# Log-sum-exp on one core: 112 rows per partition plus 16 read last, a small final store, and a logarithm held behind row 118

## Chip, cores, metric

One core of one Trainium2 chip. The metric is device microseconds of one execution; medians are over the runs of one kernel on one chip. "Column" below means one row of x in each of the 128 partitions: 128 x 4 KB, 0.524 MB. There are 128 columns.

## The reference

```python
x: [32, 512, 1024] float32, standard normal
max_x = np.max(x, axis=-1, keepdims=True)
return max_x.squeeze(-1) + np.log(np.sum(np.exp(x - max_x), axis=-1))
```

67.1 MB are read and 64 KB written. The kernel skips the maximum, sums the plain exponentials, and tests with a flag whether that was safe; the slow branch behind the flag is not taken here.

## The kernel before

Columns stream through a ring of 48. ScalarE takes the exponential. Then there are three ways to sum a column: R (VectorE reduces several columns in one instruction), T (VectorE adds the two halves and accumulates), A (ScalarE accumulates while it takes the exponential). One string of the list is one load step.

```python
B = 8                                   # columns of the second layout
W = NC - B                              # 120 rows of x, contiguous, in each partition
x_rows = x_flat[0 : P * W].rearrange("(p c) d -> p c d", p=P)
x_rest = x_flat[P * W : n].rearrange("(p c) d -> p c d", p=P)
...
loads = [
    "R8 R8", "R8 R8", "R8 R8", "R7 R6 A A", "R6 R5 A A A", "R5 R4 A", "R5 R4", "R5 T3",
    "R3 A A A", "R3 A", "R2 T2", "R3", "R1 A", "T2", "T1", "A", "A",
]
REST = 7                                # step 7 reads x_rest: columns 0 to 7
...
if following == EARLY + 14:             # logarithm of 104 columns; the scheduler places it
    nc.scalar.activation(out=res[:, 0:EARLY], in_=sumexp[:, 0:EARLY], func=AF.Ln)
if following == LATE + 3:
    check(0, LATE, 0)
...
nc.scalar.activation(out=res[:, EARLY:NC], in_=sumexp[:, EARLY:NC], func=AF.Ln)
nc.sync.dma_start(out=out_rest, in_=res[:, 0:B])        # 4 KB, early
nc.sync.dma_start(out=out_rows, in_=res[:, B:NC])       # 60 KB, last
```

## Time and profile before

| | before |
|---|---|
| device time, first measurement | 163.82 us (163.78 to 163.91) |
| span in the profile | 162.0 us |
| DMA engines busy | 97.0% |
| VectorE busy, ScalarE busy | 122.4 us, 116.8 us |
| ScalarE takes up the first and the last load | 22.04 us, 158.16 us |
| final store: issue, size | 159.58 us, 60 KB |

From the first load taken up to the last one taken up are 158.16 - 22.04 = 136.12 us, and I use this difference as the pace of the stream. What comes after 158.16 is a fixed tail. The first landing, the pace and the tail make up the span. The profile's own lines are in the prediction.

### The profile page before, as it was taken

To read this page: it belongs to the slowest core of one execution; us is meant where nothing else is said; L and a number is where in the kernel's file an instruction comes from. 1 tells how busy PE (TensorE), PEld (TensorE's weight loads), DVE (VectorE), ACT (ScalarE), POOL (GpSimd) and SP (SyncE) were. 2 spreads that over 40 slices of the span, in tenths; PEclk is the share of its full clock that TensorE was granted. 3 is DMA by queue.
4 is the path that set the end of the run, shared out by engine and by line. 5 is a ranking of instruction groups with operands and counts; after the bars stand their busy time and mean duration, and the time that the engine had idled before them with its cause. 6 is when DMAs were issued, how large, how long until landed. Compare 5 with 4: busy or idle time off the path is not lost.

```text
span 162.0 us, 216 instructions
## 1 busy us (share of the span) xinstructions
PE 0.6 (0%) x8; PEld 0.3 (0%) x8; DVE 122.4 (76%) x47; ACT 116.8 (72%) x53; POOL 0.2 (0%) x4
## 2 busy tenths in 40 slices
PE   0000000000000000000000000000000000000001
PEld 0000000000000000000000000000000000000000
DVE  0000000899949999499999995999998999979993
ACT  3000059980799609994599839999969599999993
POOL 0000000000000000000000000000000000000000
DMA  8995995996996999799999899899999999999980
GB/s 275 502 518 259 518 518 259 518 518 275 502 518 291 485 502 425 303 485 485 453 453 453 382 394 425 384 453 437 437 396 469 394 455 401 425 423 417 414 350 19
DMA packets 2818, 67.19 MB, mean 415 GB/s; under 512 B 640, under 2 KB 640, under 8 KB 1024
## 3 DMA queue, kind: packets, MB, share of 16 engines
q1 hardware_dynamic: 2816, 67.18, 97.0%
q14 instruction: 2, 0.02, 0.0%
HBM read 67.11 MB, written 0.07 MB: 415 GB/s over the span
## 4 chain that ended last, share of the span: by engine, by line
DMA 63%; DVE 22%; ACT 12%; issue 0%; SPq 0%; PE 0%; DVEq 0%; ACTq 0%
DMA ring<-in_x_dram 63%; DVE sumexp L140 21%; ACT ring L133 12%; DVE ring L145 1%; SPq L90 0%; PE count L193 0%; DVE clamped L102 0%; DVE bad L190 0%; DVE bad L189 0%; DVE clamped L106 0%; DVE fine L195 0%; PE count L194 0%; DVEq L102 0%; ACTq L133 0%
## 5 line engine op out<-in xcount | busy, mean ns | idle before, releaser
L140 DVE TENSOR_REDUCE sumexp<-ring 128x8 f32<-128x8192 f32 (+7 forms) x20 | 116.2, 5854 | 36.0 <-ACT ring L133 36.0
L133 ACT ACTIVATE ring<-ring 128x8192 f32<-128x8192 f32 (+7 forms) x24 | 101.7, 4283 | 42.0 <-DMA ring<-in_x_dram 41.9
L131 ACT ACTIVATE ring<-ring 128x1024 f32<-128x1024 f32 x12 | 12.5, 1040 | 0.0
L145 DVE SCALAR_TENSOR_TENSOR ring<-ring 128x512 f32<-128x512 f32 x8 | 5.1, 683 | 0.0
L131 ACT ACTIVATION_READ_ACCUMULATOR ring<-ring 128x1 f32 x12 | 2.2, 186 | 0.0
L77 ACT ACT_TABLE_LOAD x1 | 1.3, 1283 | 0.8 <-PEq L253 0.8
L131 ACT ACTIVATE last_exp<-ring 128x1024 f32<-128x1024 f32 x1 | 1.0, 1028 | 0.0
L110 PE MATMUL count<-far,bad 128*1 128x1 f32 x4 | 0.4, 164 | 158.8 <-DVE clamped L106 158.8
L78 DVE MEMSET ones<- 128x1 f32 x1 | 0.1, 59 | 0.9 <-PEq L253 0.9
L145 DVE DVE_READ_ACCUMULATOR ring<-ring 128x1 f32 x8 | 0.6, 81 | 0.0
L102 DVE TENSOR_SCALAR clamped<-sumexp 128x118 f32<-128x118 f32 (+1 forms) x2 | 0.4, 198 | 0.1
L106 DVE SCALAR_TENSOR_TENSOR clamped<-clamped,sumexp 128x118 f32<-128x118 f32 (+1 forms) x2 | 0.4, 224 | 0.1
L110 PEld LDWEIGHTS count<-far,bad 128*1 128x1 f32 x4 | 0.2, 80 | 158.9 <-DVE clamped L106 158.9
L195 DVE TENSOR_SCALAR fine<-count 1x1 int32<-1x1 f32 x1 | 0.1, 145 | 0.3 <-PE count L194 0.3
L162 ACT ACTIVATE res<-sumexp 128x104 f32<-128x104 f32 x1 | 0.3, 272 | 0.0
L182 ACT ACTIVATE res<-sumexp 128x24 f32<-128x24 f32 x1 | 0.2, 222 | 0.0
L189 DVE TENSOR_REDUCE bad<-ring 128x1 f32<-128x64 f32 x1 | 0.2, 219 | 0.0
L193 PE MATMUL count<-far,bad 128*1 128x1 f32 x2 | 0.2, 164 | 0.2 <-DVE bad L190 0.2
L194 PE MATMUL count<-ones,sumexp 128*1 128x1 f32 x2 | 0.2, 163 | 0.0
L131 ACT ACTIVATION_READ_ACCUMULATOR last_exp<-ring 128x1 f32 x1 | 0.2, 186 | 0.0
L190 DVE TENSOR_SCALAR bad<-bad 128x1 f32<-128x1 f32 x1 | 0.2, 153 | 0.0
L106 DVE DVE_READ_ACCUMULATOR clamped<-clamped,sumexp 128x1 f32 x2 | 0.2, 82 | 0.0
(7 smaller groups left out, 0.6 us busy)
## 6 DMA issues: line engine op xcount, KB each, us to landing
ring<-in_x_dram SPq DMA_DIRECT2D x2, 3840.0 KB, 27.7
ring<-in_x_dram SPq DMA_DIRECT2D x2, 3584.0 KB, 25.6
ring<-in_x_dram SPq DMA_DIRECT2D x1, 5120.0 KB, 31.3
ring<-in_x_dram SPq DMA_DIRECT2D x1, 4608.0 KB, 33.7
ring<-in_x_dram SPq DMA_DIRECT2D x1, 4096.0 KB, 29.3
ring<-in_x_dram SPq DMA_DIRECT2D x2, 2048.0 KB, 32.7
ring<-in_x_dram SPq DMA_DIRECT2D x1, 3072.0 KB, 36.2
ring<-in_x_dram SPq DMA_DIRECT2D x2, 1024.0 KB, 38.7
```

Source lines behind the costliest of these rows:

```text
L77: nc.scalar.preload_act_table_set("natural_log_exp_and_others")
L102: nc.vector.tensor_scalar(out=clamped[:, c0:c1], in0=sumexp[:, c0:c1], scalar1=LOW, scalar2=HIGH, op0=ALU.max, op1=ALU.min,)
L106: nc.vector.scalar_tensor_tensor(out=clamped[:, c0:c1], in0=clamped[:, c0:c1], scalar=0.0, in1=sumexp[:, c0:c1], op0=ALU.bypass, op1=ALU.n ...
L110: nc.tensor.matmul(count, lhsT=bad[:, i : i + 1], rhs=far, start=i == 0, stop=False)
L131: exp = nc.scalar.activation(out=o, in_=v, func=AF.Exp, accum_out=sums)
L133: exp = nc.scalar.activation(out=v, in_=v, func=AF.Exp)
L140: added = [nc.vector.reduce_sum(out=sums, in_=v, axis=AX.X)]
L145: nc.vector.scalar_tensor_tensor(out=lo, in0=lo, scalar=1.0, in1=ring[:, p + r, H:d], op0=ALU.mult, op1=ALU.add, accum_out=sums[:, r : r + 1],
L162: nc.scalar.activation(out=res[:, 0:EARLY], in_=sumexp[:, 0:EARLY], func=AF.Ln)
L182: nc.scalar.activation(out=res[:, EARLY:NC], in_=sumexp[:, EARLY:NC], func=AF.Ln)
L189: nc.vector.reduce_max(out=bad[:, 3:4], in_=last_row[:, 0, 0 : d // 16], axis=AX.X)
L190: nc.vector.tensor_scalar(out=bad[:, 2:3], in0=bad[:, 3:4], scalar1=LOG_LOW, scalar2=None, op0=ALU.is_lt)
```

## The change

The intent: the rows that are read last become the second layout, so that 112 columns can be stored early and only 16 in the final store. The logarithm of the 112 and the check of 118 are pinned to a place in the order of their engines. The list of loads is redrawn, and there must be a border between loads at 112.

```diff
-    B = 8
+    B = 16
-        "R8 R8", "R8 R8", "R8 R8", "R7 R6 A A", "R6 R5 A A A", "R5 R4 A", "R5 R4", "R5 T3",
-        "R3 A A A", "R3 A", "R2 T2", "R3", "R1 A", "T2", "T1", "A", "A",
+        "R6 R5 R5", "R6 R5 R5", "R8 R8", "R8 R8", "R4 R4 R3 R3 A A", "R6 T3 T3", "R6 A A", "R4 T2",
+        "R3 R3", "R3", "A A A", "R2 A", "T2", "T2", "T1", "A", "A",
...
-        if following == EARLY + 14:
-            nc.scalar.activation(out=res[:, 0:EARLY], in_=sumexp[:, 0:EARLY], func=AF.Ln)
-        if following == LATE + 3:
-            check(0, LATE, 0)
+        if c == LATE:                    # 118
+            ln = nc.scalar.activation(out=res[:, 0:W], in_=sumexp[:, 0:W], func=AF.Ln)
+            in_this_order(exp, ln)       # and ln before the next exp
+            counted = check(0, LATE, 0)  # and before the next VectorE sum
...
-    nc.sync.dma_start(out=out_rest, in_=res[:, 0:B])
-    nc.sync.dma_start(out=out_rows, in_=res[:, B:NC])
+    nc.sync.dma_start(out=out_rows, in_=res[:, 0:W])
+    nc.sync.dma_start(out=out_rest, in_=res[:, W:NC])
```

(The helper that pins an order and the slow branch's adjustments are cut.)

More of the change, by code (lines that the diff above doesn't have):

```diff
@@ L56 @@
     ENGINES = [mybir.EngineType.Activation, mybir.EngineType.DVE]
-    REST = 7
-    EARLY = 104
     LATE = 118
@@ L81, in source @@
     def source(c0, size):
-        assert c0 >= B or (c0 == 0 and size == B)
-        return x_rows[:, c0 - B : c0 - B + size, :] if c0 >= B else x_rest
+        assert c0 >= W or c0 + size <= W
+        return x_rest[:, c0 - W : c0 - W + size, :] if c0 >= W else x_rows[:, c0 : c0 + size, :]
     def load(p0, c0, size, i):
@@ L98, in without_wait, with in_this_order @@
         tc.declare_no_dep(ins.ins, group=group, reason=reason)
+    def in_this_order(first, then):
+        info = mybir.DependencyInfo(mybir.DependencyClass.NoSync, mybir.DependencyReason.DATA)
+        tc.add_manual_dep(then.ins, first.ins.name, info, reason="order on one engine")
     def check(c0, c1, i):
@@ L105, in check @@
         )
-        nc.vector.scalar_tensor_tensor(
+        counted = nc.vector.scalar_tensor_tensor(
             out=clamped[:, c0:c1], in0=clamped[:, c0:c1], scalar=0.0, in1=sumexp[:, c0:c1],
@@ L110, in check @@
         nc.tensor.matmul(count, lhsT=bad[:, i : i + 1], rhs=far, start=i == 0, stop=False)
-    following = B
+        return counted
+    ln = counted = None
+    c = 0
     p = 0
@@ L117 @@
             p = 0
-        if i == REST:
-            c = 0
-        else:
-            c = following
-            following += size
         dmas = load(p, c, size, i)
@@ L137 @@
             tc.add_to_no_dep_group("exps", exp.ins)
+            if ln:
+                in_this_order(ln, exp)
+                ln = None
             added = []
@@ L155 @@
                 tc.add_to_no_dep_group("sums", add.ins)
+                if counted:
+                    in_this_order(counted, add)
+                    counted = None
             c += s
@@ L180 @@
     nc.at_finalize(start_early)
-    nc.scalar.activation(out=res[:, EARLY:NC], in_=sumexp[:, EARLY:NC], func=AF.Ln)
-    nc.sync.dma_start(out=out_rest, in_=res[:, 0:B])
-    nc.sync.dma_start(out=out_rows, in_=res[:, B:NC])
+    nc.scalar.activation(out=res[:, W:NC], in_=sumexp[:, W:NC], func=AF.Ln)
+    nc.sync.dma_start(out=out_rows, in_=res[:, 0:W])
+    nc.sync.dma_start(out=out_rest, in_=res[:, W:NC])
     check(LATE, LAST, 1)
@@ L210 @@
                         nc.scalar.wait_ge(ready, steps)
-                    for c1, s1 in ((0, B), (B, s - B)) if c0 == 0 else ((c0, s),):
+                    edge = max(c0, min(W, c0 + s))
+                    for c1, c2 in ((c0, edge), (edge, c0 + s)):
+                        if c1 == c2:
+                            continue
                         nc.scalar.dma_start(
-                            out=ring[:, c1 - c0 : c1 - c0 + s1, :], in_=source(c1, s1)
+                            out=ring[:, c1 - c0 : c2 - c0, :], in_=source(c1, c2 - c1)
                         ).then_inc(landed, 16)
@@ L235 @@
                 nc.scalar.wait_ge(ready, steps + 2)
-                nc.scalar.dma_start(out=out_rest, in_=res[:, 0:B]).then_inc(landed, 16)
-                nc.scalar.dma_start(out=out_rows, in_=res[:, B:NC]).then_inc(landed, 16)
+                nc.scalar.dma_start(out=out_rest, in_=res[:, W:NC]).then_inc(landed, 16)
+                nc.scalar.dma_start(out=out_rows, in_=res[:, 0:W]).then_inc(landed, 16)
                 nc.scalar.wait_ge(landed, rows + 32)
```

## The prediction

> **What bounds the kernel now.** I went from the page's shares to the DMA stages, then to the last ten microseconds in order of time. The page first: each engine's busy time, the load queue, and the chain that ended last.
>
> ```profile
> span 162.0 us, 216 instructions
> PE 0.6 (0%) x8; PEld 0.3 (0%) x8; DVE 122.4 (76%) x47; ACT 116.8 (72%) x53; POOL 0.2 (0%) x4
> q1 hardware_dynamic: 2816, 67.18, 97.0%
> DMA 63%; DVE 22%; ACT 12%; issue 0%; SPq 0%; PE 0%; DVEq 0%; ACTq 0%
> ```
>
> VectorE and ScalarE have about a quarter of the span free; the 16 DMA engines have 3%, or 4.9 us, and that is the start and the end. Next, the windows view, cut where ScalarE got its next load (its columns end with GB/s).
>
> ```profile
> 22.04:41.39 19.35, 0.00 (x0) 0.00 (x0) 12.29 (x2) 13.95 (x3) 0.00 (x0) 1.00 1.00 434
> 95.89:118.87 22.98, 0.00 (x0) 0.00 (x0) 20.98 (x5) 21.70 (x12) 0.00 (x0) 1.00 0.99 428
> 135.89:154.35 18.46, 0.19 (x2) 0.09 (x2) 17.25 (x18) 18.18 (x17) 0.00 (x0) 1.00 1.00 420
> 158.16:160.30 2.14, 0.43 (x6) 0.22 (x6) 1.11 (x8) 1.37 (x4) 0.00 (x0) 1.00 0.00 0
> 160.40:160.60 0.20, 0.00 (x0) 0.00 (x0) 0.00 (x0) 0.00 (x0) 0.00 (x0) 1.00 0.72 206
> 160.60:160.80 0.20, 0.00 (x0) 0.00 (x0) 0.00 (x0) 0.00 (x0) 0.00 (x0) 1.00 0.38 101
> ```
>
> The loads run at 420 to 434 GB/s without a gap until ScalarE takes up the last one at 158.16. One column (128 rows of 4 KB, 0.524 MB) costs 19.35/16 = 1.209 us in the big loads and 18.46/15 = 1.231 us in the small ones. From 160.4 to 160.8 the final store's data moves. The tail between is a strict sequence, here from the timeline:
>
> ```profile
> 154.35 2.86 ACT L133 ACTIVATE ring<-ring 128x2048 f32<-128x2048 f32 x2 [0.24 <-DMA ring<-in_x_dram]
> 157.11 1.04 ACT L131 ACTIVATE ring<-ring 128x1024 f32<-128x1024 f32 x1
> 158.16 1.03 ACT L131 ACTIVATE last_exp<-ring 128x1024 f32<-128x1024 f32 x1
> 159.12 0.19 ACT L131 ACTIVATION_READ_ACCUMULATOR last_exp<-ring 128x1 f32 x1
> 159.34 0.22 ACT L182 ACTIVATE res<-sumexp 128x24 f32<-128x24 f32 x1
> 159.58 0.34 SPq L184 DMA_DIRECT2D out_dram<-res  x1
> 159.64 0.14 DVE L195 TENSOR_SCALAR fine<-count 1x1 int32<-1x1 f32 x1 [0.33 <-PE count L194]
> ```
>
> So the end is: last load, 1.15 us to the accumulator of its exponential, 0.25 us for the logarithm, store issued at 159.58, landed 1.6 us later (DMA issues in the page: "60.0 KB, 1.6"), span over at 162.0. The chain as printed ends in the flag test at 159.78 instead of the store, because it follows instructions; the flag's load and branch come after that, and it is done only some 0.3 us before the store has landed (the trace's semaphore records: 160.87 and 161.16), so I count it as a close second.
>
> **What the Trainium skill says.** "DMA: Bandwidth & Descriptors", section "Where 436 GB/s comes from", gives 435.2 GB/s as what the ports can take; the 434 of the big loads agrees: no arrangement of loads makes them faster. Its "Latency and other measured facts" says that a tiny transfer has a floor of about 800 ns whatever its size, and its "Specifications" that transfers under 512 B a piece are below line rate. The final store agrees with the first: 1.6 us, of which only 0.35 us has data in flight. 480 B and 64 B a row are both under 512 B, so that does not tell them apart. The same section of measured facts lists slow row pitches: 512 KiB still gives 207 GB/s against 214, 2 MiB 164. The change moves the pitch between partitions from 480 KB to 448 KB, and to 64 KB for the last sixteen columns; all are no larger than the page's mild case, so I expect no loss, but no run here has shown it.
>
> **The change, part by part.**
>
> 1. Loads. Both versions move 128 columns in 17 steps, with the same split of steps 3 to 5 among transfers and the same last five sizes (2, 2, 1, 1, 1). Between the steps of the old kernel, landing time fits 1.2045 us a column plus 0.07 us a step (estimate from the ScalarE starts: 16 columns give 19.34, and 4 give 4.89). New sum after the first step: 112 x 1.2045 + 16 x 0.07 = 136.0 us, exactly as before, since columns and steps are equal. First landing 22.02, so the last is at about 158.1 in both. Gain 0.
>
> 2. Slots of the ring. A load may be issued when VectorE has freed its 48-column ring's slots. Working the new order through with the old durations (VectorE 8.60 us for eight columns, 6.47 for six, 5.39 for five, 4.33, 3.27, 2.19; 0.61 for a T column), slots come free at 44.6, 63.9, 84.9, 95.8, 104.4 us and so on, each 9 to 30 us before the queue would run dry (60.7, 80.1, 99.4, 113.9, 123.7). Smaller first pieces free slots about 2 us earlier; with a queue that never empties that earns nothing. Gain 0.
>
> 3. Engines. VectorE: R columns 107 to 105, T columns 8 to 13, so 20 reductions and 8 additions become 21 and 13. I find six instructions more (eleven records, with accumulator reads), not the seven fewer of the description; busy time goes up about 1 us: -2.0 for the reductions (forms 8.68, 7.62, 6.55, 5.48, 4.41, 3.35, 2.28, 1.21), +5 x 0.61 = +3.1. ScalarE: A columns 13 to 10, about 1.2 us less. Neither sets the end. In the last columns my walk has VectorE finish its last addition at 158.2 (158.5 before), still ahead of ScalarE's 159.31.
>
> 4. The logarithm of 112 columns after row 118, and the check pinned there. ScalarE reaches it at about 149.4; it needs VectorE's reduction up to column 112, which my walk puts at 148.5. 0.9 us to spare, so it costs its own 0.18 us of start-to-start time (old one: 141.67 to 141.85). Afterwards ScalarE takes R2, A, T2: 149.55 + 1.82 + 1.04 + 1.82 = 154.2, against the landing of the next T2 at 154.33. It is level with the loads again, by 0.1 us. From there the sequence T2, T1, A, A is the old one: the last exponential at 158.16. Gain 0.
>
> 5. The stores. The early one (now 112 x 4 B a row, 56 KB) is issued near 149.7, but waits in the queue behind loads all issued by then, as the old one did (4.0 KB, 16.3 us to landing, that is 158.3). Its data takes about as long as the old final store's, under 0.4 us, and is gone by 158.6, a microsecond before the final store. The final store shrinks from 60 KB to 8 KB. Of its 1.6 us only the data part of 0.35 us scales: 52 KB less, at 434 GB/s, is 0.12 us; at the 150 GB/s that the old store reached (60 KB in 0.4 us) it would be 0.3 us, but the eight rows that an engine has still have a cost each. I choose 0.12. The logarithm of 16 instead of 24 columns is worth under 0.01 us. Gain 0.12.
>
> Sum: 163.82 - 0.12 = 163.70 us, or -0.07%.
>
> **Rivals.**
>
> ScalarE stalls at the pinned logarithm: if VectorE runs more than 0.9 us later than in my walk, ScalarE waits, and all but 0.1 us of the wait goes straight to the end, because the old tail has no idle ScalarE after 154.35. For it: VectorE was continuously behind in this stretch. Against it: the order of work leaves only three R3 and two T before it. A 1 us stall would make 164.6.
>
> The last sixteen columns load slower because of their 64 KB pitch. For it: nothing in the old trace reads in that pitch with 4 to 12 KB pieces. Against it: the page's figures, and the old kernel's contiguous step ran at the same 1.214 us a column as its strided neighbours. 3% on sixteen columns is 0.6 us: 164.3.
>
> The flag becomes the end: with a quicker store, the flag's branch at about 160.8 is the next wait. It would cap the gain at 0.3 us: 163.5. A full gain of a smaller store plus nothing else cannot make more than that.
>
> **Range and chances.** The old runs spread over 0.13 us, and chip and build may shift 0.2. Stall and pitch are about 1 in 8 together and cost up to 1 us; the best case is 163.4. So 163.4 to 164.1. 2% is 3.3 us. Faster by that would need bytes not moved; slower would need a rate loss of the whole stream, such as a bad 448 KB pitch: 2 in 100.
>
> **What would show it.** The chain and windows: 430 GB/s stages as before and a last exponential at 158.1 to 158.2 prove parts 1 and 2. No idle ScalarE ahead of the logarithm of 112, starting near 149.4, proves part 4. The final store's line must say 8.0 KB and about 1.5 us instead of 1.6. VectorE busy near 123.4 and ScalarE near 115.6 check part 3. I am wrong if ScalarE's last start is off by over 0.3 us, or if a gap appears in the DMA rows before 157.

## The result, and the profile after

| | before | after |
|---|---|---|
| median of 6 runs | 163.83 us (163.78 to 163.91) | 163.71 us (163.64 to 163.75) |
| ratio | 1 | 0.9992, 95% interval 0.9979 to 1.0005 |

A ratio is the mean time of one kernel's runs over that of the other's in the same rounds, so it is not quite the ratio of the medians. The 0.12 us between the medians is within the interval, although the two ranges of six runs do not overlap.

The page of the changed kernel (engine shares and load queue):

```profile
span 162.0 us, 224 instructions
PE 0.6 (0%) x8; PEld 0.3 (0%) x8; DVE 123.2 (76%) x58; ACT 116.2 (72%) x50; POOL 0.2 (0%) x4
q1 hardware_dynamic: 2816, 67.18, 96.9%
```

VectorE has eleven records more, not fewer, and 0.8 us more work; the queue is as full as before. The timeline after, from the first load and in the tail:

```profile
21.81 14.04 ACT L133 ACTIVATE ring<-ring 128x6144 f32<-128x6144 f32 x3 [19.73 <-DMA ring<-in_x_dram]
...
149.06 0.19 ACT L131 ACTIVATION_READ_ACCUMULATOR ring<-ring 128x1 f32 x1
149.15 0.28 ACT L168 ACTIVATE res<-sumexp 128x112 f32<-128x112 f32 x1
149.34 1.89 ACT L133 ACTIVATE ring<-ring 128x2048 f32<-128x2048 f32 x1
...
154.29 2.86 ACT L133 ACTIVATE ring<-ring 128x2048 f32<-128x2048 f32 x2 [0.22 <-DMA ring<-in_x_dram]
...
158.13 1.03 ACT L131 ACTIVATE last_exp<-ring 128x1024 f32<-128x1024 f32 x1
...
159.07 0.22 DVE L195 TENSOR_REDUCE bad<-ring 128x1 f32<-128x64 f32 x1 [0.42 <-issue]
...
159.55 0.34 SPq L190 DMA_DIRECT2D out_dram<-res  x1
...
159.81 0.15 DVE L201 TENSOR_SCALAR fine<-count 1x1 int32<-1x1 f32 x1 [0.33 <-PE count L200]
```

The two stores in the lists of DMA issues (KB, then us from issue to landing), of the kernel before, then of the changed one:

```profile
out_dram<-res SPq DMA_DIRECT2D x1, 60.0 KB, 1.6
out_dram<-res SPq DMA_DIRECT2D x1, 4.0 KB, 16.3
```

```profile
out_dram<-res SPq DMA_DIRECT2D x1, 56.0 KB, 8.9
out_dram<-res SPq DMA_DIRECT2D x1, 8.0 KB, 1.5
```

The pinned logarithm starts at once. ScalarE is level with the loads again at 154.29, with 0.22 us to spare. The last exponential is 0.03 us earlier than before, and so is the final store's issue. One thing is new: VectorE's small reduction has 0.42 us of "issue" ahead of it, a wait for nothing that the profile shows. The flag comes out at 159.96, not earlier, as an earlier last addition would have it, but 0.17 us later. It still does not set the end: SyncE's own semaphore records in the trace have the flag at 160.8 and the store landed at 161.08 (before: 160.87 and 161.16).

From issue to landing the final store takes 1.53 us after and 1.58 before. So this one pair of profiles shows 0.05 us of gain in the store, less than predicted, and could not settle where the 0.12 came from.

### The profile page after: what moved, and what is told of

The parts are those of the page before. It is cut to its first block, busy times and chain, and to the rows that moved or that the text cites. A ratio compares the mean times of both kernels' runs of the same rounds, so it can differ in the third digit from the quotient of the medians.

```text
span 162.0 us, 224 instructions
## 1 busy us (share of the span) xinstructions
PE 0.6 (0%) x8; PEld 0.3 (0%) x8; DVE 123.2 (76%) x58; ACT 116.2 (72%) x50; POOL 0.2 (0%) x4
## 4 chain that ended last, share of the span: by engine, by line
DMA 52%; DVE 36%; ACT 9%; issue 1%; SPq 0%; PE 0%; DVEq 0%; ACTq 0%
DMA ring<-in_x_dram 52%; DVE sumexp L143 35%; ACT ring L133 9%; DVE ring L148 1%; SPq L88 0%; DVE bad L195 0%; PE count L199 0%; DVE clamped L105 0%; DVE bad L196 0%; DVE fine L201 0%; DVE clamped L109 0%; PE count L200 0%; DVEq L195 0%; DVEq L105 0%; ACTq L133 0%
## 5 line engine op out<-in xcount | busy, mean ns | idle before, releaser
L143 DVE TENSOR_REDUCE sumexp<-ring 128x3 f32<-128x3072 f32 (+5 forms) x21 | 113.9, 5479 | 34.1 <-ACT ring L133 34.0
L133 ACT ACTIVATE ring<-ring 128x3072 f32<-128x3072 f32 (+6 forms) x27 | 104.4, 3921 | 42.5 <-DMA ring<-in_x_dram 42.5
L131 ACT ACTIVATE ring<-ring 128x1024 f32<-128x1024 f32 x9 | 9.4, 1040 | 0.0
L148 DVE SCALAR_TENSOR_TENSOR ring<-ring 128x512 f32<-128x512 f32 x13 | 8.3, 687 | 0.7 <-ACT ring L133 0.7
L131 ACT ACTIVATION_READ_ACCUMULATOR ring<-ring 128x1 f32 x9 | 1.7, 186 | 0.0
L148 DVE DVE_READ_ACCUMULATOR ring<-ring 128x1 f32 x13 | 1.1, 84 | 0.0
```

The lines of the kernel that those rows point to most:

```text
L131: exp = nc.scalar.activation(out=o, in_=v, func=AF.Exp, accum_out=sums)
L133: exp = nc.scalar.activation(out=v, in_=v, func=AF.Exp)
L143: added = [nc.vector.reduce_sum(out=sums, in_=v, axis=AX.X)]
L148: nc.vector.scalar_tensor_tensor(out=lo, in0=lo, scalar=1.0, in1=ring[:, p + r, H:d], op0=ALU.mult, op1=ALU.add, accum_out=sums[:, r : r + 1],
```

## The experiments

Twelve runs in three calls, two of them repeats; the kernel before ran beside each call (163.78, 163.70 and 163.78 us). All gave the right result. Medians are over 4 to 6 executions. Each profile is of one execution, whose time can lie about 0.2 us from the median of its run.

| run | median us (range) | ratio to before | first load, last exponential taken up at | pace |
|---|---|---|---|---|
| control | 163.71 (163.60 to 163.84) | 0.9994 | 21.95, 158.06 | 136.11 |
| store_large | 163.88 (163.79 to 164.09) | 1.0008 | 21.84, 157.98 | 136.14 |
| old_list | 163.93 (163.78 to 164.11) | 1.0006 | 22.19, 158.29 | 136.10 |
| one_pitch | 164.24 (164.20 to 164.59) | 1.0030 | 22.43, 158.65 | 136.22 |
| unpinned | 165.83 (165.74 to 166.18) | 1.0133 | tail moved | |
| early_ln | 168.49 (168.28 to 168.62) | 1.0291 | tail moved | |
| more_vector | 164.18 (163.83 to 164.36) | 1.0019 | 22.21, 158.88 | 136.67 |
| more_steps | 164.14 (164.07 to 164.38) | 1.0025 | first load split, 158.46 | |
| control_2 | 163.61 (163.50 to 163.75) | 0.9992 | 21.85, 157.97 | 136.12 |
| old_list_2 | 164.12 (164.01 to 164.23) | 1.0022 | 22.23, 158.35 | 136.12 |
| old_list_24 | 164.19 (164.17 to 164.41) | 1.0026 | 22.64, 158.74 | 136.10 |
| more_vector_16 | 164.16 (164.00 to 164.33) | 1.0023 | 22.00, 158.75 | 136.75 |

### control and control_2: the changed kernel again

No edit.

> The changed kernel unaltered, as the reference for the other runs on this chip. All theories: 163.65 to 163.75 us, 0.1 us below the kernel before; final store issued at 159.55 and landed 1.5 us later; last exponential at 158.13.

> The changed kernel once more, as the reference for this call: 163.6 to 163.8 us.

Both met in time; the first control's final store landed 1.58 us after its issue instead of 1.5. The five values of one kernel spread over 0.25 us, so steps of 0.1 us are at the limit of what can be told.

### store_large: the final store made large again

```diff
-    B = 16
+    B = 112
+    S = 112          # the logarithms stay split at 112
...
-            ln = nc.scalar.activation(out=res[:, 0:W], in_=sumexp[:, 0:W], func=AF.Ln)
+            ln = nc.scalar.activation(out=res[:, 0:S], in_=sumexp[:, 0:S], func=AF.Ln)
-    nc.scalar.activation(out=res[:, W:NC], in_=sumexp[:, W:NC], func=AF.Ln)
+    nc.scalar.activation(out=res[:, S:NC], in_=sumexp[:, S:NC], func=AF.Ln)
```

> Only the split of the stores moves: 16 columns go out early, 112 (56 KB, 448 B a row) in the final store; the logarithms stay split at 112. If the 0.12 us come from the size of the final store (my prediction), this gives them back: 163.80 to 163.85, and issue to landing rises from 1.53 to 1.58 us or more. Rival, that the size hardly matters because landing waits for something else (the one profile pair shows only 0.05 us): 163.70 to 163.77.

163.88, or 0.17 us over its control: just above what the size theory said, and off the rival. DMA issues of store_large (both stores), then of control (sizes in KB, then us from issue to landing):

```profile
out_dram<-res SPq DMA_DIRECT2D x1, 56.0 KB, 1.8
out_dram<-res SPq DMA_DIRECT2D x1, 8.0 KB, 8.6
```

```profile
out_dram<-res SPq DMA_DIRECT2D x1, 56.0 KB, 8.7
out_dram<-res SPq DMA_DIRECT2D x1, 8.0 KB, 1.6
```

The final store lands 0.19 us slower when it is large (1.77 against 1.58 us by the semaphore records), with the same pace and tail. The two ranges of run times overlap by one 0.05 us strip, so I call it shown in direction and only roughly in size.

The semaphore records of all profiles say a little more. Counted from the issue to the landing of the first of the sixteen DMA engines, the two large final stores took 1.40 us (before) and 1.41 (store_large), the twelve small ones 1.25 to 1.28: a difference of 0.12 to 0.17 us. Counted to the last engine, for which the end waits, it is 1.58 and 1.77 against 1.42 to 1.72. So the size shows, but the 60 KB store of the kernel before landed as soon as control's 8 KB did (1.58 both), and what the size is worth at the end is not settled by these records.

The layout of the loads differs too (pitch 64 KB in the first 16 columns); pace and first load show no effect of it.

### old_list, old_list_2, old_list_24: the old list with the new stores

```diff
-    B = 16
+    B = 18           # old_list_24: 24
-        "R6 R5 R5", "R6 R5 R5", "R8 R8", ...
+        "R8 R8", "R8 R8", "R8 R8", "R7 R6 A A", ...      # the whole list of before
```

> The list of loads of the kernel before, with the new stores (18 columns last, 110 early, since that list has a border at 110). My theory, that the list is worth nothing because loads land at the same pace: within 0.05 us of the control, last exponential at 158.1 to 158.2. Rival, that the new list itself made the gain: 163.8 or more.

> The old list with the new stores, unaltered, a second time; the first gave 163.93, 0.2 us over its control, where I had expected none, and its profiled run had a spread of 0.95 us between the first and last DMA engine from the first load on (control: 0.6). If that was chance (my theory now): within 0.1 us of control_2, so under 163.85. If the list itself costs: again 163.85 to 164.05.

> The old list with 104 columns a row and 24 read last: pitches 416 KB and 96 KB instead of 440 KB and 72 KB, final store 12 KB. If the pitch made old_list slow: within 0.1 us of control_2. If the list itself costs: as slow as old_list_2. If it was chance, both are at the control.

Missed, all three: none came within 0.1 us of its control. The first gave 0.22 us over its control, which I put down to chance. The repeat gave 0.51 us over control_2, with no overlap, so it is not chance. Taken by the letter, the third expectation (as slow as old_list_2) then says "the list costs". It was badly posed: it took for granted that 416 KB would be a harmless pitch. The timelines answer it. First load and last exponential of control_2, old_list_2 and old_list_24:

```profile
21.85 14.04 ACT L133 ACTIVATE ring<-ring 128x6144 f32<-128x6144 f32 x3 [19.77 <-DMA ring<-in_x_dram]
...
157.97 1.03 ACT L131 ACTIVATE last_exp<-ring 128x1024 f32<-128x1024 f32 x1
```

```profile
22.23 13.95 ACT L133 ACTIVATE ring<-ring 128x8192 f32<-128x8192 f32 x2 [20.15 <-DMA ring<-in_x_dram]
...
158.35 1.03 ACT L131 ACTIVATE last_exp<-ring 128x1024 f32<-128x1024 f32 x1
```

```profile
22.64 13.95 ACT L133 ACTIVATE ring<-ring 128x8192 f32<-128x8192 f32 x2 [20.57 <-DMA ring<-in_x_dram]
...
158.74 1.03 ACT L131 ACTIVATE last_exp<-ring 128x1024 f32<-128x1024 f32 x1
```

In these profiles the whole delay, 0.38 and 0.79 us, is there when the first load has landed, and from there on the pace is 136.1 us in all three. Up to that landing the lists do not differ: the first load is 128 pieces of 64 KB in both; only the pitch between partitions does (448, 440 and 416 KB). So the list is worth nothing, as predicted, and what is left is the pitch, which costs something; I had not predicted it in this form. How much is less sure than the profiles look: that of old_list_24 is of its slowest execution (164.41), and its median is only 0.07 us above that of old_list_2.

The landing records say where. A load is done when its last DMA engine is done: in every profile ScalarE takes up the first load 0.02 us after the last of the sixteen landings. The spread from the first engine's landing to the last one's is 0.5 us in control_2, 1.0 in old_list_2 and 1.2 in old_list_24. It is set in the first load and stays to the end. The fastest engine is at nearly the same time in all three (21.2 to 21.4 us), so it is the slowest engines that are behind, and up to the last load they do not catch up. Whether they start late or run slowly in the first load, and why the pitch should do that, is not shown. One caution: with 448 KB the profiles have the first load between 21.79 and 22.21 us and spreads of 0.35 to 0.82, so the 22.2 of 440 KB (twice) lies at the edge of that range, and only 416 KB is well outside it. That 440 KB costs rests on the ten run times of old_list and old_list_2 (medians 163.93 and 164.12, where the kernel before, with the same list at 480 KB, had 163.78) together with the unchanged pace.

### one_pitch: one layout, 512 KB

```diff
-    x_rows = x_flat[0 : P * W].rearrange("(p c) d -> p c d", p=P)
-    x_rest = x_flat[P * W : n].rearrange("(p c) d -> p c d", p=P)
+    x_rows = x_flat.rearrange("(p c) d -> p c d", p=P)
-    out_rows = out_flat[0 : P * W].rearrange("(p c) -> p c", p=P)
-    out_rest = out_flat[P * W : n].rearrange("(p c) -> p c", p=P)
+    out_all = out_flat.rearrange("(p c) -> p c", p=P)
+    out_rows = out_all[:, 0:W]
+    out_rest = out_all[:, W:NC]
```

> All 128 columns in one layout: pitch between partitions 512 KB, no separate last 16 columns; the final store then writes 64 B pieces 512 B apart. If pitch does not matter at this size: within 0.1 us of the control and big loads at 434 GB/s. If the 3% loss that the skill's page gives for 512 KiB shows in reads: 420 GB/s in the big loads, and 168 to 169 us.

164.24, between the two: 0.53 us over the control, far from the 4 to 5 us of a 3% loss in rate. The profiled execution (164.43) is 0.72 us over control's: 0.48 us are in the first load (22.43 against 21.95), 0.11 in the rest of the stream, and 0.14 in the final store, which with 64 B pieces 512 B apart took 1.72 us instead of 1.58.

### unpinned and early_ln: the place of the logarithm

```diff
 # unpinned: in_this_order does nothing; the scheduler then puts the logarithm ahead of the three A columns
+        return
 # early_ln: pinned right behind row 112
-        if c == LATE:
+        if c == W:
             ln = nc.scalar.activation(out=res[:, 0:W], in_=sumexp[:, 0:W], func=AF.Ln)
```

> The three orders on one engine are taken away, so the scheduler places the logarithm of 112 columns ahead of the three A columns. It needs VectorE's reduction of columns 109 to 111, ready at 148.2, while ScalarE comes to it at 146.0. My theory (the tail has 0.1 to 0.2 us of slack, all else goes to the end): ScalarE waits 2.2 us and the time is 165.5 to 165.9. Rival, that ScalarE catches up again behind the loads: 163.7 to 164.0.

> The logarithm of 112 columns pinned right behind the exponentials of its own columns, where ScalarE is at 143.4 and VectorE delivers at 148.2: a wait of 4.8 us. My theory: 4.6 us later than the control, 168.0 to 168.6. Rival (ScalarE catches up): under 165.

Both met: 165.83 and 168.49 us. (Without its pins unpinned also leaves the check of 118 to the scheduler; it ran at 151.83 us, in the changed kernel at 151.58.) ScalarE in the timeline of unpinned, then of early_ln:

```profile
148.39 0.30 ACT L169 ACTIVATE res<-sumexp 128x112 f32<-128x112 f32 x1 [2.14 <-DVE sumexp L144]
...
160.13 1.00 ACT L132 ACTIVATE last_exp<-ring 128x1024 f32<-128x1024 f32 x1
```

```profile
148.23 0.30 ACT L168 ACTIVATE res<-sumexp 128x112 f32<-128x112 f32 x1 [4.79 <-DVE sumexp L143]
...
162.63 1.00 ACT L131 ACTIVATE last_exp<-ring 128x1024 f32<-128x1024 f32 x1
```

Of a wait of 2.14 us, 2.07 us are left at the last exponential (160.13 against control's 158.06), and of 4.79 us 4.57 (162.63): ScalarE cannot catch up in the tail. The medians are 2.1 and 4.8 us over the control, which ran in another call, with the kernel before at 163.78 against 163.70. So the pin saves 2.1 us against what the scheduler does with this list; it gains nothing over the kernel before, where the old list let the scheduler's place do no harm.

### more_vector and more_vector_16: VectorE's instruction count

```diff
     nc.vector.memset(far, 100 * HIGH)
+    idle = stats.tile([P, 8], fp32, name="idle")          # 16 in more_vector_16
+    for k in range(8):
+        nc.vector.memset(idle[:, k : k + 1], 0.0)
```

> Eight tiny VectorE memsets at the start, where it idles until 27 us; nothing else. In the profile after, VectorE's last reduction waited 0.42 us for nothing that the profile shows, at 158.65. If that wait belongs to a place in VectorE's instruction stream, it now falls eight instructions earlier, among the last additions near 157, and the last reduction follows its predecessor at once. If it belongs to the reduction's own waits, it stays. By my theory the time is the control's in both cases (within 0.1 us), as the flag has 0.2 us to spare; rival, that the flag sets the end: over 0.1 us off the control either way.

> Sixteen tiny VectorE memsets at the start instead of eight. With eight, the instruction queue's 8 KB packet fell at 156.15 us, and the spread of that load's landings over the engines rose from 0.66 to 1.21 us. My theory (the fetch takes a DMA engine's time from the loads, and the delay stays with that engine to the end): the packet comes about eight VectorE instructions earlier, before 155 us, the spread rises there, and the time is 164.1 to 164.3 as with eight. Rival (only a fetch in the last two microseconds costs, or the memsets do): back to 163.7, or 164.6 and more.

The memsets run while VectorE idles, and yet both kernels are slower than their controls, by 0.4 and 0.5 us after the ratios. That was outside what I expected of the first. It does not come in every execution: two of the six of more_vector, 163.83 and 163.85, are at the upper edge of the control's, the other four at 164.17 to 164.36. Eight memsets more cost nothing more, so it is not their own time. Its flag is not the cause either: the last exponential itself is late, at 158.88 (0.82 us after control's; 0.26 of it is already in the first load of this profile). The DMA view of the stretch from 154 to 158.2 us has, for control:

```profile
q1 hardware_dynamic: 510, 1.36, 82.8%
```

and for more_vector:

```profile
q1 hardware_dynamic: 518, 1.43, 87.0%
q14 instruction: 1, 0.01, 0.5%
```

An 8 KB packet of the instruction queue moves while the last loads do: at 156.15 us with eight memsets, 155.56 with sixteen; in control it moves at 159.72, in the kernel before at 161.39, after the last load. In both slow kernels the spread between first and last engine jumps in the load in flight, from 0.66 to 1.21 us and from 0.58 to 1.26, and the last load keeps it. In the sorted landings of that load fifteen engines keep their distances, and one leaves the middle for the end: its share comes 0.9 us or more late, and the load is done 0.55 and 0.68 us later for it. That the packet does it is argued from the timing in these two profiles, and from the twelve others, where it moves after the last load and no jump of that size is seen; no run takes the packet away and leaves the rest. That the packet came under 155 us with sixteen was wrong, so what position in the stream calls for it is not settled.

In more_vector the reduction follows its predecessor at once, and the 0.42 us wait of the profile after is gone from there. That agrees with a wait tied to a place in VectorE's instruction stream: the profiles of the new list have it ahead of this reduction (0.42 to 0.45 us), those with memsets or with the old list do not. But its new place was not found in the trace; this stays open.

### more_steps: eight load steps more

```diff
-        "R6 R5 R5", "R6 R5 R5", "R8 R8", "R8 R8", "R4 R4 R3 R3 A A", "R6 T3 T3", "R6 A A", "R4 T2",
-        "R3 R3", "R3", ...
+        "R6", "R5", "R5", "R6", "R5", "R5", "R8 R8", "R8 R8", "R4 R4 R3 R3 A A", "R6", "T3 T3",
+        "R6", "A A", "R4", "T2", "R3", "R3", "R3", ...
-        step = {2: 4, 3: 2, 4: 2}.get(i, 1)
+        step = {6: 4, 7: 2, 8: 2}.get(i, 1)
```

> Eight load steps more: the first two loads in three pieces each and four of the middle ones in two; the last five are as before. By the fit of 1.2045 us a column plus 0.07 us a step: the last exponential 0.56 us later, 164.2 to 164.3. Rival, that only bytes count: within 0.1 us of the control.

164.14, slightly under the expectation; the ratio is 0.0031 above the control's, or 0.5 us. The last exponential is 0.40 us later than control's and 0.49 later than control_2's. Against control the fastest engine ends 0.51 us later, free of the spread: 0.064 us a step, where the fit had 0.07. Bytes alone do not decide; the rival is out. (The control ran in another call; the ratios allow for that.)

## Why the prediction was right

The measured median is 163.71 where 163.70 was predicted. Part of that is luck: the gain of 0.12 us is within the interval of the measurement, and later the same pair of kernels was 0.07 and 0.17 us apart. What holds is that nothing clear of noise was to be gained, and why.

1. **Loads, gain 0.** Right, with the best evidence of all: the pace is 136.10 to 136.14 us in before, control, control_2, store_large and all three kernels with the old list. In the one profile after it is 136.32, because one load lands 0.22 us late, at 145.63; in unpinned and early_ln a load landing at 142.0 is 0.15 and 0.31 late. control and control_2 do not show it, and its cause is not shown. The fit's cost of a step was nearly right (0.064 us instead of 0.07).
2. **Ring slots, gain 0.** Right: no gap shows in the stream, and smaller first pieces moved nothing.
3. **Engines.** VectorE busy 123.2 us (predicted 123.4). ScalarE 116.2, where 115.6 was the estimate: 0.6 us off, without effect. VectorE's last addition ends at 158.16 as walked, but the flag came later, not earlier, through the 0.42 us wait.
4. **The pinned logarithm, gain 0.** Right: no wait, 149.15 where 149.4 was walked, and 0.22 us of slack at the next T2 where 0.1 was. The rival stall was put at "all but 0.1 us"; unpinned and early_ln confirm the rule: all but 0.07 and 0.22 us of their waits were left at the last exponential.
5. **The stores, gain 0.12.** Right in direction, and the size fits: 0.17 us come back when only the stores' split is undone (the prediction's aside that 52 KB at 150 GB/s are 0.3 us should read 0.35). But the profile pair alone shows 0.05, and the first landing varies by 0.4 us among profiles with the same 448 KB pitch (21.79 to 22.21 us). How much of the 0.12 is the store and how much the new pitch against 480 KB stays open.

Of the rivals, the slow pitch was taken for a loss of rate in the last sixteen columns. That did not happen: control's last columns keep the pace. What differs with the pitch is another thing: how far apart the DMA engines are after the first load. Had the change ended at 440 KB, the small store might have been outweighed: old_list_2 is slower than the kernel before, ratio 1.0022 with an interval of 1.0008 to 1.0035 (old_list: 1.0006, with an interval that includes 1).

The change's description says "seven instructions fewer" for VectorE. Against the kernel before it has six more in the program. more_vector shows why someone would count them: with eight more, the instruction packet falls into the loads. Whether that was the reason is not shown.

None of the kernels of the experiments beats the changed one beyond the noise. With 136 us of a full queue between fixed ends, what is left are tenths.

## What to carry to other kernels

When a kernel lives off one DMA stream that never empties, split its time into first landing, pace and tail, and ask of each edit which of the three it touches; here everything but the tail and the first landing cancelled. Before giving a busy tail one more instruction, check what it waits for: a wait of 2 us there came out at the end as 2 us. And look at the DMA engine that lands last, not at the mean: where the last one fell behind here, in the first load or while an instruction packet moved, its distance to the first was still there in the last load (0.96 to 1.24 us against control's 0.59).

## What the Trainium skill lacked or had wrong

- "DMA: Bandwidth & Descriptors", section "Latency and other measured facts", row on HBM row pitch: for loads in pieces of 4 to 64 KB the 512 KiB pitch did not lower the rate by the row's 3% (207 against 214 GB/s); it added 0.48 us to the first load and 0.11 us to the 136 us after it. The row was measured on copies between HBM tensors in 16 KiB pieces, so this is a limit of its reach and not a contradiction. It has no pitches below; here 416 KB had the first load at 22.64 us where seven profiles of 448 KB had 21.79 to 22.21, and nothing in the runs says why.
- No page says that the engines' landing times come apart in the first load (0.35 to 1.26 us from the first engine to the last) and stay so while the queue is full: control_2 has 0.54 in the first load and 0.52 in the last, old_list_24 1.26 and 1.22.
- "Runtime: NRT & Kernel Launch", section "Instruction fetch mechanics", calls the cost of crossing a block of instructions mostly hidden. If the 8 KB packet of the instruction queue is such a fetch, it was not hidden here: where it moved (0.34 us) in the middle of the loads, the load in flight was done 0.55 and 0.68 us later, and the two kernels were 0.4 and 0.5 us slower. No page treats such a packet in the middle of a load stream.
- No page gives what one load step more costs behind a full SyncE queue; by the fastest engine of more_steps it is 0.064 us.
